# Log-softmax backward on one core: y of two groups as 64 KiB runs, part of the exponential through PSUM, the second group's store in halves

## Chip, core and metric

One core of a Trainium2 chip. The metric is the device time of one execution in microseconds (us). "A" is the first group of a pair, "B" the second; dyA, yA, dyB, yB are their loads. A transfer has "landed" when the last of the 16 DMA engines that share it has reported; the "lead" of a transfer is how long before the end of the transfer ahead of it it was issued.

## The reference

```
softmax_x = np.exp(y)                                  # y, dy: 8 x 1024 x 8192, fp32
sum_dy    = np.sum(dy, axis=-1, keepdims=True)
return (dy - softmax_x * sum_dy).astype(np.float32)
```

8192 rows of 8192: 268 MB each of y and dy in, 268 MB out. A group is 256 rows, two on each of 128 partitions, so a group's tensor is 8 MiB, with one contiguous run of 64 KiB in memory for each partition. There are 32 groups in 16 pairs. exp(y) is small with these inputs, so that a kernel that leaves some of the products out can still pass the comparison with the reference; the experiments say where that was done on purpose (e5 and e10 passed it; e11, which also overwrites three columns, did not).

## The kernel before

```python
SHIFT = 3840
PIECES_A = [(0, 1024), (1024, D - SHIFT), (D - SHIFT, D)]
PIECES_B = [(0, 2048), (2048, 5120), (5120, D)]
...
x_ts = [pool.tile([P, W], fp32, name=f"x{j}") for j in range(2)]     # W = 16384 columns
y_t = pool.tile([P, SHIFT + W], fp32, name="y_t")                    # one y buffer, shared
...
for b, e in pieces:                                                  # compute(), one row r
    nc.scalar.activation(y_t[:, ys], y_t[:, ys], EXP)                # in place
    nc.vector.scalar_tensor_tensor(out=x[:, xs], in0=y_t[:, ys], scalar=s_t[:, r : r + 1],
                                   in1=x[:, xs], op0=ALU.mult, op1=ALU.add)
...
for g in range(0, G, 2):
    load_dy(g, x_ts[0])
    load_y(g, SHIFT, 0, W)                       # A's y at column SHIFT
    s_t = sums(x_ts[0])
    for r in range(R):
        compute(x_ts[0], s_t, SHIFT, r, PIECES_A)
    load_dy(g + 1, x_ts[1])
    s_t = sums(x_ts[1])
    for r in range(R):
        load_y(g + 1, 0, r * D, (r + 1) * D)     # B's y at column 0, two halves: 32 KiB runs
        compute(x_ts[1], s_t, 0, r, PIECES_B)
    for j in range(2):
        nc.sync.dma_start(out=out_v[g + j], in_=x_ts[j][:])
```

The kernel has one y buffer for both groups beside the two x buffers: B's y lies over A's, which is moved by SHIFT columns, and its load must wait until A's columns there have been read. All transfers are issued from one queue, SyncE's, in order.

## Time and profile before

| | before |
|---|---|
| time, median of 3 runs | 1867.49 us (1867.17 to 1867.59) |
| span of the profiled run | 1866.1 us |
| 16 DMA engines, share of the span | 99.8% |
| VectorE, ScalarE busy | 46%, 37% |
| packets of 64 KiB, of 32 KiB | 10240, 4096 |

Read it from the DMA: it has something in flight all the time. The other two engines wait for it. The page's lines and the timeline are in the prediction.

The packet records of the trace (one entry for each packet: start, duration, bytes) are used below. The 4-byte marks among them are what each of the 16 engines writes at the end of its share of a transfer; from them come the moments at which the first engine and the last are done (the landing that the timeline shows comes some 0.4 us after the last mark). The records do not name the engine; which packet follows which on an engine is worked out from their times. A packet is called slow by what it takes over the median of its size, 2.418 us for 64 KiB; sums of slowness, and of idle time within the span, are over all packets divided by 16.

### The profile page before, as it was taken

What the parts mean: (1) busy time and instruction counts of PE and PEld (TensorE: products, weight loads), DVE (VectorE), ACT (ScalarE), POOL (GpSimd) and SP (SyncE); (2) the same over time, 40 slices, a digit from 0 to 9 for tenths busy, and PEclk for the clock granted to TensorE, in tenths of its full rate; (3) what the DMA queues carried; (4) which work ended last, traced back from release to release, by engine and by line L of the source; (5) the groups of instructions that cost most, each with busy time, mean ns of one, the idle gap of its engine ahead of it and who ended that gap; (6) DMA issues with size and microseconds to landing.
All of it is one profiled execution on the core that took longest, in us unless ns stands there. A gap on an engine that the chain in (4) does not pass through costs nothing.

```text
span 1866.1 us, 843 instructions
## 1 busy us (share of the span) xinstructions
DVE 857.9 (46%) x256; ACT 689.3 (37%) x257; POOL 0.2 (0%) x4
## 2 busy tenths in 40 slices
DVE  2907429074290742807328073280732806338163
ACT  2606326063260532605326053260523605235152
POOL 0000000000000000000000000000000000000000
DMA  9999999999999999999999999999999999999998
GB/s 427 427 427 427 431 444 429 427 434 443 427 434 438 425 435 442 428 429 431 440 431 430 438 427 436 437 440 427 430 438 435 428 437 428 438 435 434 434 428 386
DMA packets 16134, 805.36 MB, mean 432 GB/s; under 512 B 1792, under 2 KB 1792, under 8 KB 1792
## 3 DMA queue, kind: packets, MB, share of 16 engines
q1 hardware_dynamic: 16128, 805.31, 99.8%
q14 instruction: 6, 0.05, 0.0%
HBM read 536.87 MB, written 268.44 MB: 432 GB/s over the span
## 4 chain that ended last, share of the span: by engine, by line
DMA 65%; DVE 14%; another core or an unknown queue 10%; ACT 9%; issue 0%; DVEq 0%; ACTq 0%; SPq 0%
DMA x<-in_dy_dram 31%; DMA out_dram<-x 30%; DVE x L74 14%; ACT x L60 6%; ACT y_t L73 3%; DMA y_t<-in_y_dram 3%; DVEq L121 0%; ACTq L121 0%; SPq L52 0%; ACTq L73 0%; ACTq L60 0%
## 5 line engine op out<-in xcount | busy, mean ns | idle before, releaser
L74 DVE SCALAR_TENSOR_TENSOR x<-y_t,s_t,x 128x1024 f32<-128x1024 f32 (+2 forms) x192 | 579.4, 3059 | 257.5 <-ACT y_t L73 257.5
L57 DVE TENSOR_REDUCE s_t<-x 128x1 f32<-128x8192 f32 x32 | 277.8, 8682 | 721.9 <-DMA x<-in_dy_dram 721.9
L73 ACT ACTIVATE y_t<-y_t 128x1024 f32<-128x1024 f32 (+2 forms) x192 | 460.1, 2466 | 280.0 <-DMA y_t<-in_y_dram 280.0
L60 ACT ACTIVATE x<-x 128x8192 f32<-128x8192 f32 x32 | 225.0, 7030 | 863.2 <-DMA x<-in_dy_dram 863.2
L60 ACT ACTIVATION_READ_ACCUMULATOR x<-x 128x1 f32 x32 | 6.0, 187 | 0.0
L61 DVE TENSOR_SCALAR s_t<-second_t 128x1 f32<-128x1 f32 x32 | 4.6, 143 | 0.0
L60 ACT ACT_TABLE_LOAD x1 | 1.3, 1283 | 0.7 <-PEq L110 0.7
L110 POOL MEMSET const-uint8-127<- 128x1 uint8 x1 | 0.1, 102 | 0.0
L110 POOL MEMSET const-bfloat16-1.0<- 128x1 bf16 x1 | 0.1, 101 | 0.0
L110 POOL MEMSET const-float32-0.0<- 128x1 f32 x1 | 0.1, 98 | 0.2 <-issue 0.2
L110 POOL MEMSET const-float32-1.0<- 128x1 f32 x1 | 0.1, 98 | 0.0
## 6 DMA issues: line engine op xcount, KB each, us to landing
y_t<-in_y_dram SPq DMA_DIRECT2D x32, 4096.0 KB, 22.1
x<-in_dy_dram SPq DMA_DIRECT2D x32, 48.4
out_dram<-x SPq DMA_DIRECT2D x32, 32.6
y_t<-in_y_dram SPq DMA_DIRECT2D x16, 57.5
```

The costliest lines, as they stand in the source:

```text
L57: nc.vector.tensor_reduce(out=s_t[:, 0:1], in_=x[:, :D], axis=mybir.AxisListType.X, op=ALU.add, negate=True)
L60: nc.scalar.activation(x[:, D:], x[:, D:], COPY, accum_out=second_t[:])
L61: nc.vector.tensor_scalar(out=s_t[:, 1:2], in0=second_t[:], scalar1=-1.0, scalar2=None, op0=ALU.mult)
L73: nc.scalar.activation(y_t[:, ys], y_t[:, ys], EXP)
L74: nc.vector.scalar_tensor_tensor(out=x[:, xs], in0=y_t[:, ys], scalar=s_t[:, r : r + 1], in1=x[:, xs], op0=ALU.mult, op1=ALU.add,)
L110: nc = _bacc.Bacc("TRN2", target_bir_lowering=False, num_devices=1)
```

## The change

The intent: B's y in whole 64 KiB runs, as all other loads have. For that the load of yB must be let go in one piece, so A's exp of the middle 4096 columns is written to PSUM: ScalarE alone, and not VectorE, then has to be done with those columns of y. To make up for B's later start, its store goes out in halves.

```diff
-    SHIFT = 3840
+    SHIFT = 4032
+    Q = 2048
-    PIECES_A = [(0, 1024), (1024, D - SHIFT), (D - SHIFT, D)]
-    PIECES_B = [(0, 2048), (2048, 5120), (5120, D)]
+    TO = W - SHIFT                  # 12352
+    IN_PSUM = TO - 2 * Q            # 8256
+    EXP_A = [(0, 1024), (1024, 2560), (2560, 5120), (5120, IN_PSUM)]
+    EXP_A += [(IN_PSUM, IN_PSUM + Q), (IN_PSUM + Q, TO), (TO, W)]
+    EXP_B = [(0, 2048), (2048, 5120), (5120, D), (D, D + 2048), (D + 2048, D + 5120), (D + 5120, W)]
...                                  (stats in one tile; pieces may cross the two rows)
+            if b in in_psum:
+                e_t = psum.tile([P, Q], fp32, name="e_t")
+                e_ap = e_t[:, : e - b]
+            else:
+                e_ap = y_t[:, at + b : at + e]
+            nc.scalar.activation(e_ap, y_t[:, at + b : at + e], EXP)
...
+        load_dy(g, 0)
+        load_y(g, SHIFT)
+        sums(0)
+        compute(0, SHIFT, EXP_A, (IN_PSUM, IN_PSUM + Q))
+        load_dy(g + 1, 1)
+        sums(1)
+        load_y(g + 1, 0)
+        store(g, 0, 0, W)
         for r in range(R):
+            compute(1, 0, EXP_B[3 * r : 3 * r + 3], ())
+            store(g + 1, 1, r * D, (r + 1) * D)
```

More of the change, by code (lines that the diff above doesn't have):

```diff
@@ L36 @@
     assert N == G * P * R and D == 8192 and G % 2 == 0
-    SHIFT = 3840
-    PIECES_A = [(0, 1024), (1024, D - SHIFT), (D - SHIFT, D)]
-    PIECES_B = [(0, 2048), (2048, 5120), (5120, D)]
+    SHIFT = 4032
[5 more added lines that the diff above has]
+    EXP_B = [(0, 2048), (2048, 5120), (5120, D), (D, D + 2048), (D + 2048, D + 5120), (D + 5120, W)]
+    assert D <= IN_PSUM
     y_v = y.flatten_outer_dims().rearrange("(g p r) d -> g p (r d)", p=P, r=R)
@@ L46 @@
     pool = ctx.enter_context(tc.tile_pool(name="pool", bufs=1))
-    stats = ctx.enter_context(tc.tile_pool(name="stats", bufs=3))
+    psum = ctx.enter_context(tc.tile_pool(name="psum", bufs=2, space=bass.MemoryType.PSUM))
     x_ts = [pool.tile([P, W], fp32, name=f"x{j}") for j in range(2)]
     y_t = pool.tile([P, SHIFT + W], fp32, name="y_t")
-    def load_dy(g, x):
-        nc.sync.dma_start(out=x[:], in_=dy_v[g])
-    def sums(x):
-        s_t = stats.tile([P, R], fp32, name="s_t")
-        second_t = stats.tile([P, 1], fp32, name="second_t")
+    stats = pool.tile([P, 8], fp32, name="stats")
@@ L57, in sums, with load_dy, load_y, store @@
+    def load_dy(g, j):
+        nc.sync.dma_start(out=x_ts[j][:], in_=dy_v[g])
+    def load_y(g, at):
+        nc.sync.dma_start(out=y_t[:, at : at + W], in_=y_v[g])
+    def store(g, j, lo, hi):
+        nc.sync.dma_start(out=out_v[g][:, lo:hi], in_=x_ts[j][:, lo:hi])
+    def sums(j):
+        x, c = x_ts[j], 4 * j
         nc.vector.tensor_reduce(
-            out=s_t[:, 0:1], in_=x[:, :D], axis=mybir.AxisListType.X, op=ALU.add, negate=True
+            out=stats[:, c : c + 1], in_=x[:, :D], axis=mybir.AxisListType.X, op=ALU.add, negate=True
@@ L59, in sums @@
         )
-        nc.scalar.activation(x[:, D:], x[:, D:], COPY, accum_out=second_t[:])
+        nc.scalar.activation(x[:, D:], x[:, D:], COPY, accum_out=stats[:, c + 2 : c + 3])
         nc.vector.tensor_scalar(
-            out=s_t[:, 1:2], in0=second_t[:], scalar1=-1.0, scalar2=None, op0=ALU.mult
-        )
-        return s_t
-    def load_y(g, at, lo, hi):
-        nc.sync.dma_start(out=y_t[:, at + lo : at + hi], in_=y_v[g][:, lo:hi])
-    def compute(x, s_t, at, r, pieces):
+            out=stats[:, c + 1 : c + 2],
+            in0=stats[:, c + 2 : c + 3],
+            scalar1=-1.0,
+            scalar2=None,
+            op0=ALU.mult,
+        )
@@ L70, in compute @@
+    def compute(j, at, pieces, in_psum):
+        x = x_ts[j]
         for b, e in pieces:
-            xs = slice(r * D + b, r * D + e)
-            ys = slice(at + r * D + b, at + r * D + e)
-            nc.scalar.activation(y_t[:, ys], y_t[:, ys], EXP)
-            nc.vector.scalar_tensor_tensor(
-                out=x[:, xs],
-                in0=y_t[:, ys],
-                scalar=s_t[:, r : r + 1],
-                in1=x[:, xs],
-                op0=ALU.mult,
-                op1=ALU.add,
-            )
@@ L83 @@
-    for g in range(0, G, 2):
-        load_dy(g, x_ts[0])
-        load_y(g, SHIFT, 0, W)
-        s_t = sums(x_ts[0])
-        for r in range(R):
-            compute(x_ts[0], s_t, SHIFT, r, PIECES_A)
-        load_dy(g + 1, x_ts[1])
-        s_t = sums(x_ts[1])
-        for r in range(R):
-            load_y(g + 1, 0, r * D, (r + 1) * D)
-            compute(x_ts[1], s_t, 0, r, PIECES_B)
-        for j in range(2):
-            nc.sync.dma_start(out=out_v[g + j], in_=x_ts[j][:])
+            if b in in_psum:
[3 more added lines that the diff above has]
+                e_ap = y_t[:, at + b : at + e]
@@ new lines, in compute @@
+            nc.scalar.activation(e_ap, y_t[:, at + b : at + e], EXP)
+            for r in range(R):
+                lo, hi = max(b, r * D), min(e, (r + 1) * D)
+                if lo < hi:
+                    nc.vector.scalar_tensor_tensor(
+                        out=x[:, lo:hi],
+                        in0=e_ap[:, lo - b : hi - b],
+                        scalar=stats[:, 4 * j + r : 4 * j + r + 1],
+                        in1=x[:, lo:hi],
+                        op0=ALU.mult,
+                        op1=ALU.add,
+                    )
```

## The prediction

> **What bounds the kernel now.** I read the page from the DMA rows outward, because no compute engine is half full: VectorE is busy 46% of the span and ScalarE 37%. The first view is the page itself, its header, slices and queue parts.
>
> ```profile
> span 1866.1 us, 843 instructions
> DVE 857.9 (46%) x256; ACT 689.3 (37%) x257; POOL 0.2 (0%) x4
> ...
> DMA  9999999999999999999999999999999999999998
> ...
> DMA packets 16134, 805.36 MB, mean 432 GB/s; under 512 B 1792, under 2 KB 1792, under 8 KB 1792
> ...
> q1 hardware_dynamic: 16128, 805.31, 99.8%
> ```
>
> The 16 DMA engines have packets for 99.8% of the span, in every slice. The packet count says what they move: 16128 less the 1792 under 512 B (16 for each of 112 transfers: their completion marks) leaves 14336 data packets, which is 80 transfers of 128 runs of 64 KiB (10240) and 32 of 128 runs of 32 KiB (4096). The 32 KiB runs are the two half-width y loads of each second group.
>
> The second view is the timeline of the first pair of groups; then the same load of y in the last pair.
>
> ```profile
> 22.47 7.03 ACT L60 ACTIVATE x<-x 128x8192 f32<-128x8192 f32 x1 [20.46 <-DMA x<-in_dy_dram]
> ...
> 41.80 14.32 ACT L73 ACTIVATE y_t<-y_t 128x1024 f32<-128x1024 f32 x6 [12.21 <-DMA y_t<-in_y_dram]
> ...
> 49.47 9.25 SPq L67 DMA_DIRECT2D y_t<-in_y_dram  x2
> 61.15 7.03 ACT L60 ACTIVATE x<-x 128x8192 f32<-128x8192 f32 x1 [5.02 <-DMA x<-in_dy_dram]
> 62.41 8.68 DVE L57 TENSOR_REDUCE s_t<-x 128x1 f32<-128x8192 f32 x1
> 62.52 30.76 SPq L95 DMA_DIRECT2D out_dram<-x  x2
> ...
> 70.88 7.21 ACT L73 ACTIVATE y_t<-y_t 128x2048 f32<-128x2048 f32 x3 [2.61 <-DMA y_t<-in_y_dram]
> ...
> 81.56 7.21 ACT L73 ACTIVATE y_t<-y_t 128x2048 f32<-128x2048 f32 x3 [3.47 <-DMA y_t<-in_y_dram]
> ```
>
> ```profile
> 1806.51 7.03 ACT L60 ACTIVATE x<-x 128x8192 f32<-128x8192 f32 x1 [4.97 <-DMA x<-in_dy_dram]
> ...
> 1816.22 7.22 ACT L73 ACTIVATE y_t<-y_t 128x2048 f32<-128x2048 f32 x3 [2.59 <-DMA y_t<-in_y_dram]
> ...
> 1825.98 7.22 ACT L73 ACTIVATE y_t<-y_t 128x2048 f32<-128x2048 f32 x3 [2.54 <-DMA y_t<-in_y_dram]
> ```
>
> Each line that ends a wait for a load gives the moment of its landing. Three 8 MiB loads land at 22.47, 41.80 and 61.15: 19.33 and 19.35 us apart. The two y halves of 4 MiB take 9.73 and 10.68 us in the first pair, 9.71 and 9.76 us in the last. So the engines go from one transfer straight into the next; the waits of ScalarE and VectorE are waits for a saturated DMA, and their idle time costs nothing. The trace has 96 transfers' worth of 8 MiB; at 19.33 us that is 1855.7 us. The span is 1866.1, so only 10.4 us (0.6%) of anything else exists: about 2 us before the first packet (the first landing, 22.47, is 3.1 us more than 19.33, part of it slower first packets), some 2 to 4 us for the halves, and the rest engines that finish apart. In the packet records the last transfer's completion marks are spread over 4.5 us from the first engine to the last.
>
> **What the Trainium skill says.** "DMA: Bandwidth & Descriptors", section "Where 436 GB/s comes from": the ports between the DMA engines and SBUF cap at 435.2 GB/s. The trace agrees: 8 MiB (8.389 MB) in 19.33 us is 434.0 GB/s, so a full-width transfer has nothing left to win. The same page, "Why small descriptors are slow (HBM only)": a fixed cost for each packet, quoted for small ones. The packet records agree in kind: 64 KiB took 2.418 us and 32 KiB 1.215 us in the median, so two halves cost 12 ns more than one whole; over 16 pairs, 16 half runs on each engine a pair, that is an estimate of 1.5 us in all. "Perfetto Trace Analysis", section "Identifying the Most-Contended Engine": work on the engine that is most contended first; here that is the DMA, and the change takes no byte off it. "VectorE: DVE Perf Modes", section "Why PSUM operands drop a tier": fp32 with a PSUM operand runs at 1x. No PSUM operand is in this trace; the SBUF instruction already takes about 1.04 ns an element (2.351 us for 2048, 3.415 for 3072), so I expect no change from PSUM.
>
> **The change, part by part.** *Bytes and packets.* The y load of the second group goes from two 4 MiB halves to one 8 MiB transfer; its store goes from one 8 MiB transfer to two halves. Still 112 transfers, 10240 packets of 64 KiB and 4096 of 32 KiB: the 32 KiB runs move from HBM reads to HBM writes. If a written 32 KiB run costs what a read one does, the gain is zero. If it costs nothing extra, the gain is what the halves cost now: in the last pair 9.71 + 9.76 - 19.33 = 0.14 us, times 16 is 2.2 us, and about 1.5 us more from the slow second halves of the first two pairs (10.68, and 10.23 by the same lines of the second pair, against 9.7). So 0 to 4 us, of which I take about 1.5.
>
> *Order of transfers in a pair.* Before: dyA, yA, dyB, yB first half, yB second half, store A, store B. After: dyA, yA, dyB, yB, store A, store B first half, store B second half. The DMA stays full if each is issued before its predecessor ends. I lay this on the clock of the first pair, with ScalarE at 0.19 us + 0.834 ns an element and VectorE at 0.21 us + 1.042 ns, fitted to the rows of 1024 to 3840 columns (1.048 to 3.387 us and 1.281 to 4.211 us).
>
> - yA lands at 41.8. ScalarE's pieces of 1024, 1536, 2560, 3136, 2048, 2048 take 1.05 + 1.48 + 2.33 + 2.80 + 1.91 + 1.91: it is through column 12352 at 53.3. VectorE's pieces start at 42.9, are held up by ScalarE twice, and end at 44.2, 46.2, 49.6 and 53.3 (3072 and 64 columns of the fourth). The load of yB overwrites what these two have read: the last two pieces go to PSUM so that their VectorE half need not be waited for. Both conditions come true at 53.3, so yB is issued at about 53.4, where the first half went at 49.47 before. dyB ends at 61.1: 7.7 us to spare. The first transfer's issue to its first packet took some 1.4 us, so this holds by some 6 us. Without PSUM the wait would be for 53.3 + 2 x 2.35 = 58.0, 3.1 us before dyB ends, or 1.7 after that start time.
> - VectorE goes on with 2.35 + 2.35 + 4.41 (4032 columns) to 62.4; store A is issued then, as before (62.52), and is needed at 80.5.
> - yB lands at 61.15 + 19.34 = 80.5 whole, while before its first half landed at 70.88. VectorE's first half of B is done at 80.5 + 1.95 + 2.35 + 2 x 3.42 = 91.6; store A ends at 99.9, so the first half store has 8 us. The second half is done 9.2 us later, at 100.9; the first half store ends at 109.5, 8.6 us to spare.
> - dyA of the next pair waits for store A's landing (99.9) and stands in the queue behind the last store: issued at about 101.4, needed at 119.2. yA needs B's arithmetic, done. dyB waits for both half stores (119.2) and is needed at 158.
>
> The thinnest of these margins is 6 us, and it repeats in each of 16 pairs. No wait turns into a DMA gap.
>
> *Arithmetic.* A pair has the same columns in more pieces: 13 exp against 12, and 14 VectorE products against 12, since the fourth piece crosses from the first row's sum to the second's at column 8192 and leaves 64 columns over. At the fixed 0.19 and 0.21 us of an instruction that is 16 x 0.19 = 3 us on ScalarE and 32 x 0.21 = 7 us on VectorE, all beside the DMA. On the path: nothing, since the end too is set by the DMA (store B is queued well before store A ends).
>
> *Sum.* 1867.5 measured before, less about 1.5: 1866.
>
> **Rivals.** (1) *The later landing of yB makes the DMA run dry.* VectorE and ScalarE lose 9.7 us of head start in the second group. For it: the arithmetic of B, 20 us, now starts only when store A starts. Against: two half stores instead of one, the first due 8 us before it is needed. If I were wrong by a whole margin plus 2 us in each pair, 16 x 2 = 32 us: 1899, 1.7% slower. Unlikely. (2) *The release of yB comes late*, because PSUM operands run slower or the dependency is taken for the whole tile. If the load had to wait for all of A, 62.4, against 61.1 less 1.4: a gap of 2.7 us a pair, 43 us in all, 1909 (2.2% slower). Against: the wait lists of the built kernel show this load waiting on ScalarE and VectorE counts and one earlier transfer; and before, the same tile let the half loads go after a part of the pieces (49.47, while the pieces ran on to 62.5). (3) *Stores in 32 KiB runs cost more than loads in them*, or the turn from load to store gets worse: the slow packets of the first pairs sit at the end of the second half load, just before the stores begin. If each pair kept a 1 us loss there, +16 us: 1883, still within 2%. (4) *Full gain*, 4 us: 1863.
>
> **Range and chances.** The total is pinned between 1855.7 + 3 us of start (1859) and the present time unless a gap opens; the margins say none does. Executions of the kernel before agree within 0.4 us. I put 8 in 10 on 1862 to 1870. Faster by over 2% (under 1830) is below the bandwidth bound: 1%, for an error of mine. Slower by over 2% (over 1905) needs rival 2: 2%. Within 2%: 97%.
>
> **What would show it.** Right: 16128 packets on the queue again at 99.7 to 99.9%; yB issued 11.6 us after yA lands and some 7 us before dyB lands; yB landing 19.3 us after dyB; two half store issues about 9.3 us apart; VectorE on PSUM at 2.35 us for 2048. Wrong: a digit under 9 in the DMA row inside the span, a landing interval for a whole load above 20 us, or the queue's wait for VectorE at the store of A or B ending after the transfer ahead of it has landed.

## The result and the profile after

| | before | changed |
|---|---|---|
| time, median of 4 runs | 1867.33 us (1866.91 to 1867.59) | 1867.1 us (1866.93 to 1867.71) |
| span of the profiled run | 1866.1 us | 1865.8 us |

The ratio is 1.000 (95% interval 0.9982 to 1.0017). Ratios here are the mean time of one kernel's fast runs over that of the other's of the same rounds, so not quite the ratio of the medians. The change did nothing to the time.

The page of the changed kernel, the lines that answer to those of before:

```profile
span 1865.8 us, 920 instructions
DVE 860.6 (46%) x288; ACT 689.0 (37%) x273; POOL 0.2 (0%) x4
...
DMA  9999999999999999999999999999999999999998
...
DMA packets 16135, 805.37 MB, mean 432 GB/s; under 512 B 1792, under 2 KB 1792, under 8 KB 1792
...
q1 hardware_dynamic: 16128, 805.31, 99.8%
...
L96 DVE SCALAR_TENSOR_TENSOR x<-e_t,stats,x 128x2048 f32<-128x2048 f32 x32 | 73.7, 2345 | 0.0
...
L92 ACT ACTIVATE e_t<-y_t 128x2048 f32<-128x2048 f32 x32 | 58.5, 1858 | 0.0
```

The same packets, the same share, the same digits. 2048 columns take VectorE 2.345 us out of PSUM (2.351 out of SBUF before) and ScalarE 1.858 us into PSUM (1.910 into SBUF before).

The timeline of its first pair:

```profile
41.84 7.36 ACT L92 ACTIVATE y_t<-y_t 128x1024 f32<-128x1024 f32 x4 [12.21 <-DMA y_t<-in_y_dram]
...
52.85 4.60 DVE L96 SCALAR_TENSOR_TENSOR x<-e_t,stats,x 128x2048 f32<-128x2048 f32 x2
53.02 0.33 SPq L64 DMA_DIRECT2D y_t<-in_y_dram  x1
...
61.18 7.03 ACT L75 ACTIVATE x<-x 128x8192 f32<-128x8192 f32 x1 [4.92 <-DMA x<-in_dy_dram]
...
61.81 40.40 SPq L67 DMA_DIRECT2D out_dram<-x  x3
...
81.58 14.32 ACT L92 ACTIVATE y_t<-y_t 128x2048 f32<-128x2048 f32 x6 [13.28 <-DMA y_t<-in_y_dram]
...
86.18 15.67 DVE L96 SCALAR_TENSOR_TENSOR x<-y_t,stats,x 128x3072 f32<-128x3072 f32 x5 [0.30 <-ACT y_t L92]
102.26 0.60 SPq L61 DMA_DIRECT2D x<-in_dy_dram  x1
```

yB is issued at 53.02, 11.2 us after yA landed and 8.2 us before dyB has landed (61.18). yB is in at 81.58, 20.4 us after dyB and not 19.3; the packet records show why below. VectorE ends B at 86.18 + 15.67 = 101.85 and the next pair's dyA goes out at 102.26.

Now the tenth pair of the same kernel; the line at 1109.78 is dyB's landing, that at 1129.07 yB's:

```profile
1090.44 7.36 ACT L92 ACTIVATE y_t<-y_t 128x1024 f32<-128x1024 f32 x4 [12.22 <-DMA y_t<-in_y_dram]
...
1101.60 0.33 SPq L64 DMA_DIRECT2D y_t<-in_y_dram  x1
...
1109.78 7.03 ACT L75 ACTIVATE x<-x 128x8192 f32<-128x8192 f32 x1 [4.93 <-issue]
...
1129.07 1.91 ACT L92 ACTIVATE y_t<-y_t 128x2048 f32<-128x2048 f32 x1 [12.16 <-DMA y_t<-in_y_dram]
```

Here yB takes 19.29 us, as any whole load. Nothing is lost in the middle of the run.

### The profile page after: what moved, and what is told of

Same layout as the page of the kernel before. It is cut to its first block, busy times and chain, and to the rows that moved or that the text cites. A ratio compares the mean times of both kernels' runs of the same rounds, so it can differ in the third digit from the quotient of the medians.

```text
span 1865.8 us, 920 instructions
## 1 busy us (share of the span) xinstructions
DVE 860.6 (46%) x288; ACT 689.0 (37%) x273; POOL 0.2 (0%) x4
## 3 DMA queue, kind: packets, MB, share of 16 engines
q1 hardware_dynamic: 16128, 805.31, 99.8%
## 4 chain that ended last, share of the span: by engine, by line
DMA 56%; DVE 18%; ACT 12%; another core or an unknown queue 10%; issue 2%; SPq 0%; ACTq 0%; DVEq 0%
DMA x<-in_dy_dram 30%; DMA y_t<-in_y_dram 26%; DVE x L96 18%; ACT y_t L92 6%; ACT x L75 6%; SPq L67 0%; ACTq L142 0%; DVEq L142 0%; SPq L61 0%; SPq L64 0%; ACTq L92 0%; ACTq L75 0%
## 5 line engine op out<-in xcount | busy, mean ns | idle before, releaser
L96 DVE SCALAR_TENSOR_TENSOR x<-y_t,stats,x 128x1024 f32<-128x1024 f32 (+2 forms) x192 | 511.1, 2704 | 396.1 <-ACT y_t L92 394.7
L72 DVE TENSOR_REDUCE stats<-x 128x1 f32<-128x8192 f32 x32 | 277.9, 8683 | 589.9 <-DMA x<-in_dy_dram 589.9
L92 ACT ACTIVATE y_t<-y_t 128x3072 f32<-128x3072 f32 (+6 forms) x176 | 403.7, 2362 | 393.6 <-DMA y_t<-in_y_dram 393.6
L96 DVE SCALAR_TENSOR_TENSOR x<-e_t,stats,x 128x2048 f32<-128x2048 f32 x32 | 73.7, 2345 | 0.0
L92 ACT ACTIVATE e_t<-y_t 128x2048 f32<-128x2048 f32 x32 | 58.5, 1858 | 0.0
L76 DVE TENSOR_SCALAR stats<-stats 128x1 f32<-128x1 f32 x32 | 4.6, 145 | 0.0
## 6 DMA issues: line engine op xcount, KB each, us to landing
out_dram<-x SPq DMA_DIRECT2D x32, 4096.0 KB, 18.3
out_dram<-x SPq DMA_DIRECT2D x16, 38.2
```

Of the source, the lines that this page charges most:

```text
L72: nc.vector.tensor_reduce(out=stats[:, c : c + 1], in_=x[:, :D], axis=mybir.AxisListType.X, op=ALU.add, negate=True)
L76: nc.vector.tensor_scalar(out=stats[:, c + 1 : c + 2], in0=stats[:, c + 2 : c + 3], scalar1=-1.0, scalar2=None, op0=ALU.mult,)
L92: nc.scalar.activation(e_ap, y_t[:, at + b : at + e], EXP)
L96: nc.vector.scalar_tensor_tensor(out=x[:, lo:hi], in0=e_ap[:, lo - b : hi - b], scalar=stats[:, 4 * j + r : 4 * j + r + 1], in1=x[:, lo:hi ...
```

## The experiments

The theory at the start: the DMA engines are the bound, and each part of the change lies beside them. Rivals: gains of the longer reads are cancelled by losses of the shorter writes; the late start of B costs and something else pays for it; arithmetic holds the DMA up by a little everywhere. Each edit below is against the changed kernel, and each time is compared with it (1867.1) or with the kernel before of the same rounds.

**e1: no 32 KiB run at all.**

```diff
-            store(g + 1, 1, r * D, (r + 1) * D)      # in the loop over r
+        store(g + 1, 1, 0, W)                         # after it
```

> The changed kernel with the second group's store as one 8 MiB transfer again, so no run of 32 KiB is left. Theory (the DMA engines are full all along; short runs cost some 12 ns each pair of halves): within 2 us of the changed kernel, 1865 to 1867.5; landings of whole loads 19.3 to 19.5 us apart. Rival (32 KiB stores cost what the 64 KiB y loads gained, so gain and loss cancel): 1863 to 1865, 2 to 4 us faster than both kernels.

Measured: 1934.7 us, ratio to before 1.0362 (1.0347 to 1.0376). Both expectations missed. The timeline of its first pair, and its queue line:

```profile
82.26 14.32 ACT L92 ACTIVATE y_t<-y_t 128x2048 f32<-128x2048 f32 x6 [13.52 <-DMA y_t<-in_y_dram]
...
86.86 15.67 DVE L96 SCALAR_TENSOR_TENSOR x<-y_t,stats,x 128x3072 f32<-128x3072 f32 x5 [0.30 <-ACT y_t L92]
102.55 0.34 SPq L67 DMA_DIRECT2D out_dram<-x  x1
```

```profile
q1 hardware_dynamic: 13824, 805.31, 97.8%
```

The whole store of B can go only when VectorE is through all of B, 86.86 + 15.67 = 102.53. It went at 102.55. By the packet records the engines ended store A between 100.37 (the first) and 101.25 (the last), and nothing else could move: dyA of the next pair needs store A landed, and stands behind store B in the queue. The engines stood idle for 2.4 to 3.6 us in each pair. So the halves of the store are not a detail of run length: without them the whole load of yB costs 68 us.

**e10: the same with the cause removed.** The last two products of B are left out, which lets the whole store go earlier. Its output is wrong, which doesn't matter for the time.

```diff
+        store(g + 1, 1, 0, W)                         # whole, as in e1
-                if lo < hi:
+                if lo < hi and not (j == 1 and lo > D):
```

> Wrong result on purpose: y and the store of the second group both whole, as in the run that took 1934.7, but without the last two VectorE products of B. The store of B can then be issued at about 95.5 on the first pair's clock, 5 us before store A ends at 100.7, in place of 102.2. Theory (the 68 us of the run with the whole store were its late issue): 1865 to 1869, and no gap at store B. Rival (64 KiB stores behind 64 KiB loads are slow in themselves): 1920 to 1940.

Measured: 1867.14 us, ratio to before 0.9999 (0.9984 to 1.0013). The same two views:

```profile
86.21 9.01 DVE L96 SCALAR_TENSOR_TENSOR x<-y_t,stats,x 128x3072 f32<-128x3072 f32 x3 [0.30 <-ACT y_t L92]
95.25 0.34 SPq L67 DMA_DIRECT2D out_dram<-x  x1
```

```profile
q1 hardware_dynamic: 13824, 805.31, 99.9%
```

Issued at 95.25, the whole store costs nothing. e1's 68 us were the late issue. It also says that with no run of 32 KiB left the time is 1867 all the same: what run length gives is too small for these timings to show.

**e2: the y halves back, the store halves kept.**

```diff
-        load_y(g + 1, 0)
+        for h in range(2):                            # each half: W // 2 columns, 32 KiB runs
+            nc.sync.dma_start(out=y_t[:, h * W // 2 : ...], in_=y_v[g + 1][:, h * W // 2 : ...])
```

> The changed kernel with y of the second group again as two 32 KiB-run loads, the store split kept: 4096 more packets of 32 KiB. Theory: 1867 to 1869; the half loads land 9.71 to 9.75 us apart in the middle of the run, as before, and the half stores stay at 9.68 by their completion marks. Rival (cancelling): 1869 to 1871, as the loss of the loads comes back and the loss of the stores stays.

Measured: 1868.06 us, ratio to before 1.0006 (0.9993 to 1.0019). In the theory's range, and not to be told apart from no change. Cancelling gains and losses of 2 to 4 us, the first rival, are not seen: neither putting both in halves nor (e10) both whole moves the time by 2 us.

**e5: no arithmetic.** All of sums() and compute() removed, the transfers left in their order. Its output is wrong, which doesn't matter for the time.

```diff
-        sums(0)
-        compute(0, SHIFT, EXP_A, (IN_PSUM, IN_PSUM + Q))
-        sums(1)
-            compute(1, 0, EXP_B[3 * r : 3 * r + 3], ())
```

> Wrong result on purpose: the changed kernel's transfers in their order and sizes, with no arithmetic at all (dy is stored as it was loaded), so the only waits are those of transfers on transfers. Theory (arithmetic is wholly beside the DMA): 1864 to 1868, the same as the changed kernel. Rival (some of the 10 us over the sum of the transfers is waiting for arithmetic or its SBUF traffic slowing the transfers): 1857 to 1861.

Measured: 1866.46 us, ratio to before 0.9996 (0.9982 to 1.0011). The changed kernel runs as fast as its bare transfers, to within this interval, and the kernel before as fast as it (the bare transfers of that one were not run). The third rival is out at the size that it was given, 5 us or more.

**e3 and e8: a later release of y.** Fewer of A's pieces through PSUM: none in e3, only the second in e8.

```diff
-        compute(0, SHIFT, EXP_A, (IN_PSUM, IN_PSUM + Q))
+        compute(0, SHIFT, EXP_A, ())                  # e3
+        compute(0, SHIFT, EXP_A, (IN_PSUM + Q,))      # e8
```

> The changed kernel with all exp pieces in place, so that the load of yB also waits for VectorE on the two pieces that went through PSUM. Theory: yB is issued at about 57.5 on the first pair's clock in place of 53.0, still 3.6 us before dyB lands at 61.2: no gap, 1866 to 1868. Rival (the release of y is what the change is worth): yB lands later than 19.5 us after dyB in all pairs, some 2 to 4 us in each, 1900 to 1930.

> The changed kernel with only the second of the two middle pieces through PSUM, so that the load of yB waits for one VectorE product more than in the changed kernel and one less than with none through PSUM. It is issued at about 55.2 on the first pair's clock, 5.9 us before dyB has wholly landed (7.7 to 8 in the changed kernel, 3.6 with none, which cost 28 us). Theory (a load must be issued about one 64 KiB packet, 2.4 us, plus 1.4 us of start before the first of the 16 DMA engines runs out, and the engines finish a transfer up to 5 us apart): in between, 1868 to 1876. Rival (a step: 4 us of lead is enough or nothing): 1866 to 1868.

Measured: e3 1895.0 us, ratio 1.0149 (1.0135 to 1.0163). e8 1869.73 us (1867.55 to 1878.61 in four runs), ratio 1.0022 (0.9997 to 1.0046). e3 missed the theory, and lies 5 us under the rival's range. e8's median is in the theory's range, but its interval includes no change at all, so that the rival, a step, is not ruled out by time; in its trace the slow packets add up to 2.3 us more than in the changed kernel, some 1.5 us of that in the yB of the last three pairs. The timeline of e3 in its tenth pair:

```profile
1105.05 14.41 ACT L92 ACTIVATE y_t<-y_t 128x1024 f32<-128x1024 f32 x7 [12.20 <-DMA y_t<-in_y_dram]
...
1120.70 0.33 SPq L64 DMA_DIRECT2D y_t<-in_y_dram  x1
1124.35 7.03 ACT L75 ACTIVATE x<-x 128x8192 f32<-128x8192 f32 x1 [4.89 <-DMA x<-in_dy_dram]
...
1145.41 14.32 ACT L92 ACTIVATE y_t<-y_t 128x2048 f32<-128x2048 f32 x6 [13.94 <-DMA y_t<-in_y_dram]
```

yB was issued at 1120.70, 3.65 us before dyB had wholly landed at 1124.35; still it came in at 1145.41, 21.06 us later, not 19.29. The share of the DMA engines hides this loss, since a slow packet counts as busy:

```profile
q1 hardware_dynamic: 16128, 805.31, 99.7%
```

A landing is that of the last engine. The packet records give the others, as the lead of yB's issue over the first and the last engine's end of dyB:

| | first pair: over first engine / last | last pair | time |
|---|---|---|---|
| changed | 7.34 / 7.79 us | 2.13 / 7.35 us | 1867.1 |
| e8, one piece | 4.86 / 5.51 | 1.44 / 5.41 | 1869.7 |
| e3, no piece | 2.74 / 3.27 | 0.86 / 3.22 | 1895.0 |

The 16 engines end a transfer 0.45 us apart in the first pair of the changed kernel and 5.2 us apart in its last: single packets are slow by up to 0.8 us now and then, and nothing in this run brings the engines together again. The lead over the last engine stays what the arithmetic makes it; the lead over the first melts away. It does not order the losses alone: e3's first pair, with all engines between 2.74 and 3.27 us, already had yB's first packets slow by 0.33 us in the mean, the changed kernel's last pair, where the first engine had 2.13 us and the last 7.35, by 0.10.

**e4: the load of yB waits for all of A.**

```diff
-        load_y(g, SHIFT)
+        load_y(g, 0)
-        compute(0, SHIFT, EXP_A, (IN_PSUM, IN_PSUM + Q))
+        compute(0, 0, EXP_A, (IN_PSUM, IN_PSUM + Q))
```

> The changed kernel with the first group's y put at column 0, so that the load of yB overlaps all of it and waits for the whole first group. Theory: yB is issued at about 62.1, 1 us after dyB has landed, and its first packet follows 1.4 us later: a gap of 2.3 us in each of 16 pairs, 1904 (1895 to 1915), yB landing 21.5 to 22.5 us after dyB in every pair, the DMA's share near 98%. Rival (there is slack elsewhere in the pair that takes it up): under 1880.

Measured: 1936.22 us, ratio 1.0373 (1.0357 to 1.0389), above the range: 69 us where the gaps alone were to make 37. The tenth pair, with dyB's landing, yB's issue and yB's landing 23.9 us after dyB (21.5 to 22.5 were expected):

```profile
1147.25 7.03 ACT L75 ACTIVATE x<-x 128x8192 f32<-128x8192 f32 x1 [4.86 <-DMA x<-in_dy_dram]
...
1147.94 0.33 SPq L64 DMA_DIRECT2D y_t<-in_y_dram  x1
...
1171.16 14.32 ACT L92 ACTIVATE y_t<-y_t 128x2048 f32<-128x2048 f32 x6 [16.79 <-DMA y_t<-in_y_dram]
```

So a late transfer costs more than its gap. In the packet records two more costs stand out: the first packet of the late yB on each engine (3.1 us in the mean in place of 2.418), and, some 17 us later, the last packets of yB just before store A begins.

**e11: a late transfer without arithmetic.** Transfers as in e5, and four VectorE copies of one column make yB wait for dyB. Its output is wrong, which doesn't matter for the time.

```diff
         load_dy(g + 1, 1)
+        for t in (y_t[:, 0:1], x_ts[0][:, 0:1], x_ts[1][:, 0:1], x_ts[1][:, D : D + 1]):
+            nc.vector.tensor_copy(out=t, in_=x_ts[1][:, 5:6])
```

> Wrong result on purpose: transfers alone, but the load of yB waits for dyB's landing (by four VectorE copies of one column), so it is late in each pair and all 16 engines start it together; no other arithmetic runs. Theory (a late transfer costs its gap of 2 to 2.5 us, 0.7 us of slow first packets and 1.2 us at the next turn from load to store, since the engines are in step there again): 16 x 4.2 less the 2 us that the turns cost anyway, 1925 to 1936. Rival (the slow packets at the turn come from arithmetic on SBUF at the same time): only the gap and first packets, 1908 to 1918.

Measured: 1930.08 us, ratio 1.0336 (1.032 to 1.0351). The theory's size; arithmetic has no part in it. The three costs, each from the packet records, over the kernel named:

| | idle engines | slow first packets of the late transfer | slow packets at turns | sum | measured |
|---|---|---|---|---|---|
| e3 over changed | 5.28 - 2.95 = 2.3 | 8.2 | 19.1 - 2.5 = 16.6 | 27.1 | 27.9 |
| e4 over changed | 43.52 - 2.95 = 40.6 | 10.6 | 19.3 - 2.5 = 16.8 | 68.0 | 69.1 |
| e11 over e5 | 37.51 - 2.55 = 35.0 | 10.9 | 19.7 - 2.2 = 17.5 | 63.4 | 63.6 |

(The 2.5 to 3 us of idle time that all share is for the most part the start and the end of the program.) In e3 the engines hardly ran dry: almost all of its loss is slow packets. A turn is the change from the loads to store A; e1's sum closes in the same way: 40.4 idle, 1.2 in first packets, 14.0 at the turn to store A and 12.4 at the turn from store B back to dyA make 68.0, against 67.6 measured. In an undisturbed kernel the turn is dear once: 0.90 us in the first pair of the changed kernel (most of what makes yB's 20.4 us above), 0.16 in the second, about 0.1 later and 0.37, first packets included, in the last. With a late transfer it is dear in every pair: 1.1 to 1.4 us in e4 and e11, 0.6 to 1.3 in e3. My word for it in the expectation of e11, that the engines are "in step" there, does not hold: in e3 they were 2 to 3 us apart and the turn cost as much, while in the changed kernel's second pair they were 0.49 us apart and it cost 0.16. Why a late transfer brings it back stays open.

**e6 and e7: run length, magnified.** yB as eight loads of 8 KiB runs and store B whole (e6); yB whole and store B as eight stores of 8 KiB runs (e7).

```diff
+        for h in range(8): nc.sync.dma_start(out=y_t[:, h * W // 8 : ...], in_=...)      # e6
+        store(g + 1, 1, 0, W)                                                            # e6, after the loop over r
+            for h in range(4): store(g + 1, 1, r * D + h * Q, r * D + (h + 1) * Q)       # e7
```

> The changed kernel with y of the second group as eight loads of 8 KiB runs and its store as one of 64 KiB runs. It magnifies the cost of short read runs: 7 more packets for each 64 KiB. If a read packet costs 8 ns more than its bytes, as 2 x 1.215 against 2.418 us says, 16 pairs x 8 runs x 7 x 8 to 12 ns = 7 to 11 us: 1873 to 1878. Rival (the cost sat in the turn from load to store and not in run length): 1866 to 1868.

> The changed kernel with the second group's store as eight stores of 8 KiB runs. It magnifies the cost of short written runs. Theory: the half stores took 2 x 9.68 us by their completion marks against 19.32 for a whole one, 0.04 us a pair for one more packet for each run of 64 KiB; seven more are 0.28 us a pair, 4.5 us in all: 1870 to 1873, less than reads of the same length cost. Rival (stores cost as loads): 1873 to 1878.

Measured: e6 1873.11 us, ratio 1.0032 (1.0017 to 1.0047); e7 1875.88 us, ratio 1.0046 (1.0029 to 1.0063). e6 is at the foot of what the theory said, e7 above it. In the packet records the median read of 8 KiB took 312 ns and the median write 309 ns, against 2418 / 8 = 302 for its part of a long run: 10 and 7 ns a packet. Over 16 pairs x 8 runs x 8 packets that is 10 us and 6.9 us. For the reads this is more than the time rose (6.0 us over the changed kernel): packet times overlap there and add up to 100.1% of the span. The completion marks measure it without that, in the second to seventh pairs, where the engines are still close together: eight loads took 19.86 to 19.91 us where a whole load in the changed kernel took 19.35 to 19.54, eight stores 19.62 to 19.66 where a whole store (e10) took 19.32. That is some 0.45 us a pair for reads, 7 us in all, and 0.31 for writes, 5 us in all. So writes are the cheaper ones, as the theory had it, and e7's time is not made by them alone: its packets at the turn were slow by 5.9 us in place of 2.5. Why, I have no run for. For the halves of 32 KiB the medians give 1.5 us in the whole kernel before (2 x 1.215 against 2.418) and 1.0 us in the changed one (2 x 1.213): half a microsecond apart, which no timing here could see.

**e9: an attempt at a faster version, stores from ScalarE's queue.**

```diff
-        nc.sync.dma_start(out=out_v[g][:, lo:hi], in_=x_ts[j][:, lo:hi])
+        nc.scalar.dma_start(out=out_v[g][:, lo:hi], in_=x_ts[j][:, lo:hi])
-            store(g + 1, 1, r * D, (r + 1) * D)       # in the loop over r
+        for r in range(R): store(g + 1, 1, r * D, (r + 1) * D)      # after B's exp
```

> The changed kernel with its stores issued from ScalarE's queue in place of SyncE's (A's after ScalarE's sum of A and its exp, B's two after all of B's exp), so that loads and stores stand in two queues. Theory (the DMA engines are the bound whichever queue feeds them; at most the 2 to 3 us of slow packets at the turn from load to store may go): 1863 to 1868. Rival (queues mix reads and writes and the loads land later, which shortens the lead of yB's load): over 1875.

Measured: 1969.05 us, ratio 1.0543 (1.0526 to 1.0561), the rival's side, and far beyond it. The queue's own waits, changed kernel first, then e9, and e9's queues:

```profile
SPq L61 <- DMA out_dram<-x: 246.8, 17, 17.2
```

```profile
SPq L61 <- DMA out_dram<-x: 1378.0, 33, 53.5
```

```profile
q1 hardware_dynamic: 9216, 536.88, 65.2%
q10 hardware_dynamic: 6912, 268.44, 31.5%
```

The columns of the first two are total us, number, longest. SyncE waited 1378 us, not 247, for stores to land before it could issue the next load of dy. A store now shares the engines with the loads issued beside it: store A landed 44.1 us after its issue in the median, not 38.2, and a half store 35.2, not 18.3. In the first pair yB landed at 98.30, not 81.58. ScalarE itself was held back by its stores only once (6.0 us). So the x buffers come free later, and the engines are down to 65.2% + 31.5%. That the scarce buffers are the whole of it is argued from these waits and not tested; with them, one queue in the right order was the better plan. No version tried beats the two kernels.

## Why the prediction was right

The time (1866 said, 1867.1 measured) and its reason held: the DMA bound is the same before and after, and every wait that the change lengthens ends before the DMA needs it. e5 shows the bound directly. How thin the waits are was read wrongly, as the fourth and fifth points say. Point by point:

- *Packets and share.* 16128 packets at 99.8%, as said.
- *The order of events.* yB's issue 53.4 said, 53.02 seen; store A 62.4 and 61.81; VectorE's end of B 100.9 and 101.85, since yB landed 1.1 us late, 0.9 of it at the first turn; next dyA 101.4 and 102.26. PSUM left VectorE's rate alone.
- *The gain of 0 to 4 us, taken as 1.5.* Mis-sized: 0.2 us by the medians, nothing that can be told from zero. The 1.5 us of slow second halves in the first pairs was put down to run length; it was the turn from load to store, and came back with whole loads (0.90 us in the first pair). What run length really gave, 32 KiB packets of 1.213 us in place of 1.215, is within the noise.
- *"The thinnest of these margins is 6 us, and it repeats in each of 16 pairs."* Wrong, and without harm to the time only by luck: nothing in the prediction said that the lead would shrink. The margin was worked out from landings, which are the last engine's. Over the first engine the lead falls from 7.34 us to 2.13 us in the last pair, where yB's slow packets already came to 0.37 us. The start of a transfer that was taken off, 1.4 us, is also misread: the first load was issued at 0.73 us and its first packet began at 1.74, so it is 1.0 us (the expectation of e8 repeats the 1.4).
- *"Without PSUM ... 3.1 us before dyB ends, or 1.7 after that start time"*: taken as just enough; e3 lost 28 us with 3.65 us before dyB's landing. The part of the change that looked like a reserve is needed; with one of its two pieces (e8) the loss was 2.6 us in the median, not clear of the noise.
- *The half stores.* Their 8 us was about right (the first was issued at 92.95, 7.1 us before the first engine ended store A at 100.02), but the prediction did not ask what a whole store would do. In e1 it was issued 2.2 us after the first engine had ended store A, and cost 68 us.
- *"A landing interval for a whole load above 20 us"*, a sign of being wrong, did come: 20.40 us in the first pair. It was no effect of the change: before it, the two halves of that load took 9.73 + 10.68 = 20.41 us.
- *Rivals.* Running dry, in the form of a late store or a late release, is real and was priced too low: the 2.7 us gap a pair of the second rival was to cost 43 us, and e4, with such a gap, lost 69.

The Trainium skill was a good guide to the bound: its 435.2 GB/s ("DMA: Bandwidth & Descriptors", section "Where 436 GB/s comes from") is what a whole load reaches within 0.3%, and in e5 the transfers alone take as long as the kernel.

## What to carry to other kernels

Where the DMA engines are full, a rearrangement of arithmetic, buffers and run lengths has little to win (nothing that could be measured here) and can cost; read each part of such a change as a lead over the moment when the *first* DMA engine runs out too, and not only over the landing, which is the last one's. Look at that lead late in the run, after the engines have drifted apart, and do not trust the DMA share alone: e3 lost 28 us at 99.7%. A transfer that is late pays its gap, slow first packets, and slow packets at the next turn, so that here 2.5 us of gap cost 4.3 us a pair (e4).

## What the Trainium skill lacked or had wrong

- "DMA: Bandwidth & Descriptors", section "Why small descriptors are slow (HBM only)", gives the mechanism and an example at 256 B, and no size at long runs. Here the packet records give 10 ns a packet read and 7 ns written at 8 KiB, 6 ns read and 4 ns written at 32 KiB (1215 and 1213 against 2418 / 2); the 10 ns overstate the cost, as packets overlap.
- The same page, "Rules for kernel authors", says of spreading DMAs over SP, ACT and GpSimd for bandwidth that it doesn't help. It can hurt: stores on a second queue cost 102 us (1969.05 against 1867.52), with later landings, and buffers that came free later as the likely reason (not tested).
- The same page, "Where 436 GB/s comes from", says that for transfers between HBM and SBUF the HBM side, some 358 GB/s, binds. Here, with one core running, it did not: a whole load ran at 434.0 GB/s (8 MiB in 19.33 us).
- No page has how far the 16 engines drift apart: 0.45 us apart at the end of a transfer in the first pair, 5.2 us in the last, so a landing says little of when the first engine runs out.
- No page says how early a transfer must be issued to follow without loss: leads of 0 to 2.7 us over the first engine lost 1.74 us a pair (e3); leads of 3.4 to 7.2 us in the changed kernel, from its second pair to its fifteenth, lost nothing beyond the 0.02 to 0.2 us at the turn.
- No page has the cost of the turn from loads to stores: 0.9 us once, 0.1 us later, 0.6 to 1.4 us in each pair with a late load.
